# A decoder layer's block products: sums in the PSUM banks, pairs interleaved, left factors split three products ahead

## The chip, the cores and the metric

The kernel runs on one core of a Trainium2 chip. The metric is the device time of one execution in microseconds. The core has five engines with instruction queues of their own: TensorE (PE in the profile, its weight loads PEld), VectorE (DVE), ScalarE (ACT), GpSimd (POOL) and SyncE (SP), which here only issues transfers. TensorE writes its results to PSUM, eight banks of 128 x 512 f32; VectorE and ScalarE read and write PSUM, GpSimd does not in this kernel.

## The reference

One layer of a hybrid decoder on 1024 tokens of 1024 channels in f32, then a last RMS norm. What matters here, cut down:

```python
h = rmsnorm(x, norm_mix);  u = h @ w_in            # 1024 x 11264 columns, split by branch
od = diff_attention(dq, dk, dv, lam);  o_r = silu(rg) * group_norm(retention(rq, rk, rv))
o_l = rg_lru_branch(lx, ...) * gelu(ly)
g = sigmoid(gates)
merged = g[0] * (od @ w_branch[0]) + g[1] * (o_r @ w_branch[1]) + g[2] * (o_l @ w_branch[2])
x = x + merged @ w_out
x = x + cross_attention(rmsnorm(x), mem)
x = x + square(relu(rmsnorm(x) @ mlp_w1)) @ mlp_w2
return rmsnorm(x)
```

## The kernel before

Every f32 operand of a matrix product is held as the sum of two parts in the format f32r, "hi" and "lo" (`split`, L70 and L71: ScalarE casts hi, another engine subtracts to get lo). A product of two such operands is three matmuls into one PSUM bank, hi x hi, hi x lo and lo x hi (`mm3`, L59 to L61).

The kernel runs in stages: retention; differential attention; then the stage of `h_products`; the three branches' products (`branch`); the output projection (`w_out`); cross-attention; the first MLP product (`mlp_in`, `mlp1`), whose squared ReLU and the sums of its blocks go to DRAM; the second MLP product (`mlp2`).

`h_products`, `branch` and `mlp1` compute their results as 2 x 2 block products with seven multiplications instead of eight (Winograd's form). A **pair** is two weight units of 128 output channels: its four left blocks A11, A12, A21, A22 are [128, 512] each (four k-tiles of 128 channels), the right factors are blocks [128, 4, 512] of the activations, B11, B21, B22 and their sums T1 to T4, held split in SBUF in the pools slotA and slotB. The left sums are S1 = A21 + A22, S3 = A11 - A21, S2 = S1 - A11, S4 = A12 - S2 (`left`, L1067, four VectorE instructions). The products are

P1 = A11 B11, P2 = A12 B21, P3 = S4 B22, P4 = A22 T4, P5 = S1 T1, P6 = S2 T2, P7 = S3 T3,

each 4 x 3 = 12 matmuls of 512 columns, and the results C11 = P1 + P2; with U2 = P1 + P6, U3 = U2 + P7, U4 = U2 + P5: C21 = U3 + P4, C22 = U3 + P5, C12 = U4 + P3. There are 23 pairs in `h_products` (retention's gate "rg", eight LRU pairs "lru", the merge gates "gate"; from the third pair on LRU pairs and others take turns until the LRU pairs are used up), four in each of three branches, and 16 in `mlp1`: 51 pairs.

`product` takes a bank of its own for each of the seven products from six banks that take turns (`p6`). ScalarE copies P1 to the SBUF buffer t0 (L1122), VectorE makes U2, U3 and U4 in t0 and t1 (L1126, L1128, L1131) as soon as their terms are there, and `emit` gets each result block as a sum x + y still to be made: in `h_products` VectorE adds (L676) and ScalarE applies GELU or SiLU where wanted; in `branch` VectorE adds (L810), multiplies by the sigmoid of the gate (L811) and adds the sum of the branches before (L813), with the gate and that sum loaded by SP (L804, L808); in `mlp1` VectorE adds (L1147) and squares the ReLU (L1155).

The left unit of a product is split where the product is traced (`pair_unit`): hi by ScalarE, lo by GpSimd, but by VectorE for P6 and P4 in `branch` and for the first two pairs of `mlp1`. The left sums are made once P1 and P2 are traced. The raw units are loaded when P1 is traced. The order of products is ORDER = 1, 2, 6, 7, 5, 4, 3 one pair after the other, or BY_BLOCK = 1, 2, 3, 7, 6, 5, 4, which takes two pairs product by product: the first two and the last two pairs of `h_products`, pairs 2 and 3 of each branch, the first two of `mlp1`. While pairs 2 and 3 of a branch run, the right blocks of the next branch replace those that have had their last use (`load_blocks`, `fill_block`, L775: transfer, cast, lo on VectorE).

LRU pairs also run a convolution (L614, L616), the gate products with ScalarE's sigmoids, tanh, exponential and square root, and a scan on VectorE (L639 to L642). `o_sums` (L749) makes block sums of the branches' inputs on VectorE from and to DRAM.

The order within each engine's queue is made by the tile planner when the program is built: it takes the traced order as priority and its own costs of instructions to decide what is ready; `after` fixes the order of instructions that share a key, such as all casts of left units ("wsplit") and all weight loads ("wdma"). On the chip each queue is worked off in order.

```python
    def p6(self, psum):
        return lambda: psum.tile([P, HB], F32, tag="p", name="ps1", bufs=6)
```

## Time and profile before

| | |
|---|---|
| time, median of 3 executions | 2488.87 us (2486.42 to 2490.97) |
| the profiled execution's span | 2489.1 us, 31236 instructions |
| TensorE busy | 2355.3 us (95%), 11132 matmuls |
| VectorE, ScalarE, GpSimd busy | 1851.9, 1042.4, 1088.3 us (74%, 42%, 44%) |
| block products on TensorE | from 754.9 to 1556.2 and from 1821.2 to 2143.5 us; 4284 matmuls |
| bytes moved by transfers | 334.08 MB, mean 134 GB/s |

The span runs from the first to the last instruction of the profiled execution; the page gives no other time for that execution. Matmuls overlap their successors, so "busy" of TensorE is the union of rows that are each longer than the distance between two starts. In the rows of groups, "out<-in" are the program's names of tiles: `ps` a product's bank, `wu` a left unit, `block` a right factor, `sf` and `st` raw units, sums and t0, t1 in `h_products` and `branch`, `ut` and `sraw` the same in `mlp1`, `y` a branch's result, `hab` the MLP's.

### The profile page before, as it was taken

The page shows a single profiled execution, that of the slowest core. Times are in us where ns is not written, and L with a number is a line of the kernel's source. Part 1 is how long each engine was busy: PE and PEld are TensorE (multiplying, and loading weights), DVE is VectorE, ACT ScalarE, POOL GpSimd, SP SyncE. Part 2 cuts the span into 40 slices and gives each one's busy share as a digit, 9 for nine tenths or more (in the row PEclk, how much of TensorE's full clock was granted, in tenths as well). Part 3 has the DMA queues.
Part 4 walks back from the last instruction along what each step waited for, and adds up shares of the span by engine and source line. Part 5 has one row for each costly group of instructions (what it writes and reads, how often), then busy time and mean ns, then how long its engine had stood idle before and what let it go on. Part 6 is the DMA issues. An engine that isn't in the chain of part 4 may idle for free. (4 is left out here: it accounts for less than half of the span.)

```text
span 2489.1 us, 31236 instructions
## 1 busy us (share of the span) xinstructions
PE 2355.3 (95%) x11132; PEld 1906.0 (77%) x11132; DVE 1851.9 (74%) x2850; ACT 1042.4 (42%) x1823; POOL 1088.3 (44%) x714
## 2 busy tenths in 40 slices
PE   9999999999999999999998978899989999999996
PEld 7888878787876877777776767688768888778884
DVE  7577476767786777777677887534788888878888
ACT  5443344545455554454354443235442222343333
POOL 1122212221214555565553333225145555698787
PEclk9999999999999999999999989999999999999999
DMA  5222212122114435534576776434225444744432
GB/s 173 74 85 69 62 45 60 44 60 54 51 41 140 152 120 185 182 119 144 194 233 220 241 264 205 141 129 136 94 85 178 148 140 140 275 152 169 147 142 75
DMA packets 137259, 334.08 MB, mean 134 GB/s; under 512 B 17152, under 2 KB 27393, under 8 KB 137104
## 3 DMA queue, kind: packets, MB, share of 16 engines
q1 hardware_dynamic: 136528, 330.25, 40.2%
q8 instruction: 89, 1.46, 0.3%
q10 hardware_dynamic: 576, 1.84, 0.2%
q14 instruction: 66, 0.54, 0.1%
HBM read 229.21 MB, written 98.63 MB: 132 GB/s over the span
## 5 line engine op out<-in xcount | busy, mean ns | idle before, releaser
L59 PE MATMUL ps<-block,wu 128*128 128x512 f32 x1428 | 570.5, 400 | 55.6 <-DVE sf L1126 23.5
L61 PE MATMUL ps<-block,wu 128*128 128x512 f32 x1428 | 568.2, 398 | 16.7 <-POOL wu L71 10.2
L60 PE MATMUL ps<-block,wu 128*128 128x512 f32 x1428 | 565.0, 396 | 0.1
L71 POOL TENSOR_TENSOR wu<-st,wu 128x512 fp32r<-128x512 f32 x214 | 324.9, 1533 | 323.4 <-ACT wu L70 323.3
L59 PEld LDWEIGHTS ps<-block,wu 128*128 128x128 f32 x1428 | 273.2, 191 | 120.0 <-issue 19.6
L61 PEld LDWEIGHTS ps<-block,wu 128*128 128x128 f32 x1428 | 272.9, 191 | 85.5 <-POOL wu L71 15.8
L60 PEld LDWEIGHTS ps<-block,wu 128*128 128x128 f32 x1428 | 272.7, 191 | 60.7 <-DVE block L71 1.1
L70 ACT CAST wu<-st 128x512 fp32r<-128x512 f32 x240 | 141.5, 618 | 163.3 <-DVE st L1067 68.9
L59 PE MATMUL ps<-wu,hu 128*128 128x512 f32 x448 | 176.6, 394 | 15.6 <-DVE acc L1199 13.6
L71 POOL TENSOR_TENSOR w<-st,w 128x1024 fp32r<-128x1024 f32 x50 | 122.1, 2453 | 154.9 <-ACT w L70 137.5
L61 PE MATMUL ps<-wu,hu 128*128 128x512 f32 x448 | 174.9, 392 | 5.1 <-DVE hu L71 5.1
L60 PE MATMUL ps<-wu,hu 128*128 128x512 f32 x448 | 175.2, 391 | 0.1
L1199 DVE TENSOR_TENSOR acc<-acc,ps 128x512 f32<-128x512 f32 x216 | 137.8, 677 | 21.3 <-PE ps L61 20.6
L71 POOL TENSOR_TENSOR wu<-sf,wu 128x512 fp32r<-128x512 f32 x63 | 115.9, 1853 | 64.9 <-ACT wu L70 51.8
L71 DVE TENSOR_TENSOR hu<-sth,hu 128x1024 fp32r<-128x1024 f32 x56 | 122.1, 2185 | 20.6 <-ACT hu L70 20.2
L467 ACT ACTIVATE p<-sc,mx 128x256 f32<-128x256 f32 (+7 forms) x128 | 94.5, 740 | 65.8 <-DVE mx L464 61.9
L59 PEld LDWEIGHTS ps<-wu,hu 128*128 128x128 f32 x448 | 84.6, 189 | 38.9 <-DVE acc L1199 10.7
L59 PE MATMUL psk<-block,w 128*128 128x512 f32 x256 | 104.8, 409 | 0.0
L61 PEld LDWEIGHTS ps<-wu,hu 128*128 128x128 f32 x448 | 84.6, 189 | 23.5 <-DVE hu L71 6.0
L61 PE MATMUL psk<-block,w 128*128 128x512 f32 x256 | 101.8, 398 | 0.0
L60 PE MATMUL psk<-block,w 128*128 128x512 f32 x256 | 101.6, 397 | 0.0
L60 PEld LDWEIGHTS ps<-wu,hu 128*128 128x128 f32 x448 | 84.6, 189 | 17.8 <-POOL wu L71 0.5
(391 smaller groups left out, 5627.2 us busy)
## 6 DMA issues: line engine op xcount, KB each, us to landing
sth<-h SPq DMA_DIRECT2D x56, 512.0 KB, 8.9
st<-in_w SPq DMA_DIRECT2D x32, 512.0 KB, 4.3
h<-hab SPq DMA_DIRECT2D x32, 512.0 KB, 2.8
w<-in_w SPq DMA_DIRECT2D x8, 2048.0 KB
sgb<-gsp SPq DMA_DIRECT2D x48, 256.0 KB, 4.3
gsp<-l SPq DMA_DIRECT2D x44, 256.0 KB, 3.1
acc<-y SPq DMA_DIRECT2D x40, 256.0 KB, 4.2
st<-in_w_br SPq DMA_DIRECT2D x18, 512.0 KB, 6.4
```

The lines of the kernel that those rows point to most:

```text
L59: nc.tensor.matmul(ps, lhsT=lhs.hi, rhs=rhs.hi, start=start, stop=False)
L60: nc.tensor.matmul(ps, lhsT=lhs.hi, rhs=rhs.lo, start=False, stop=False)
L61: nc.tensor.matmul(ps, lhsT=lhs.lo, rhs=rhs.hi, start=False, stop=stop)
L70: ins = self.nc.scalar.copy(dst.hi, src)
L71: self.lo_ins = (lo_engine or self.nc.vector).tensor_tensor(dst.lo, src, f32(dst.hi), op=ALU.subtract)
L467: nc.scalar.activation(p[:, 0:n], sc[:, 0:n], AF.Exp, bias=mx, accum_out=l)
L1199: eng.tensor_tensor(acc[k][:, st, :], acc[k][:, st, :], x if isinstance(x, bass.AP) else acc[x][:, st, :], op=ALU.add)
```

## The change

- **Banks.** A pair has three banks instead of seven. P1 and P2 share bank X, so that it holds C11; P6, P7 and P4 share Y; P5 and P3 share Z. ScalarE copies P1 out of X to t0 before P2 is added. VectorE adds t0 to P6 in its bank (U2), ScalarE copies U2 to t0; P7 is added by TensorE (U3), ScalarE copies U3 to t1; P4 is added (C21). Z plus t1 is C22, and with P3 added to Z, Z plus t0 is C12. So `emit` gets C11 and C21 without a second term; ScalarE copies them out (in `mlp1` with ReLU and Square), and in `branch` the product with the gate reads the bank.
- **Order.** ORDER is 1, 6, 2, 5, 7, 4, 3. Neighbouring pairs overlap: P4 and P3 of a pair stand behind P1 of the next (SLOT, `overlapped`). Pairs taken product by product follow ORDER.
- **Splits ahead.** `play` prepares (loads, splits, sums) each left unit three products before its product is run. The sums S1, S3, S2 are made behind the split of A11, S4 behind that of A12, in place of the raw blocks. Lo is made on VectorE for five products, on GpSimd for P4 and P3. The next pair's raw units are loaded when P6 is prepared.
- **The rest that follows.** The T blocks of h are loaded in the order T2, T1, T3, T4, the branches' right blocks in the new ORDER; the LRU's gate products are done in two halves, behind P4 and P3 of the next pair, and use the banks of the other pool; `o_sums` stand behind P4; GpSimd makes the last add in `branch`; the last branch's blocks and the two `hx` of the output projection lie in other slots; in `mlp1` the second raw unit lies in `sraw`. The first two pairs of `mlp1` keep the old order and a bank a product (`product_apart`).

```diff
-    def mmk(self, ps, pairs):
+    def mmk(self, ps, pairs, onto=False):
         n = len(pairs)
+        kw = {"skip_group_check": True} if onto else {}
         for i, (l, r) in enumerate(pairs):
-            self.mm3(ps, l, r, i == 0, i == n - 1)
+            self.mm3(ps, l, r, i == 0 and not onto, i == n - 1, **kw)
...
-    ORDER = (1, 2, 6, 7, 5, 4, 3)
-    BY_BLOCK = (1, 2, 3, 7, 6, 5, 4)
+    ORDER = (1, 6, 2, 5, 7, 4, 3)
+    SLOT = {1: 0, 6: 3, 2: 4, 5: 5, 7: 6, 4: 8, 3: 9}
+    def overlapped(self, pairs):
+        return [x[1:] for x in sorted((7 * p + s, p, k) for p in pairs for k, s in self.SLOT.items())]
+    def play(self, seq, prep, run, ahead=3):
+        for i in range(-ahead, len(seq)):
+            if i + ahead < len(seq):
+                prep(*seq[i + ahead])
+            if i >= 0:
+                run(*seq[i])
...
+    def left_part(self, k, c, eng):
+        w, tt = c["w"], lambda o, x, y, op: eng.tensor_tensor(o, x, y, op=op)
         if k == 1:
+            tt(c["s1"], w["A21"], w["A22"], ALU.add)
+            w["S1"], w["S2"], w["S3"] = c["s1"], w["A11"], w["A21"]
+            tt(w["S3"], w["A11"], w["A21"], ALU.subtract)
+            tt(w["S2"], c["s1"], w["A11"], ALU.subtract)
+        elif k == 2:
+            w["S4"] = w["A12"]
+            tt(w["S4"], w["A12"], w["S2"], ALU.subtract)
...
+    def prepare(self, k, c, lo):
+        c["u", k] = self.pair_unit(c["w"][self.LEFT[k]], lo)
+        self.left_part(k, c, self.nc.vector)
...
+    BANK = {1: "X", 2: "X", 6: "Y", 7: "Y", 4: "Y", 5: "Z", 3: "Z"}
+    def product(self, k, c, right, psum, emit, apart=False):
+        u, r, b = c["u", k], right[self.RIGHT[k]], self.BANK[k]
+        onto = b in c
+        if not onto:
+            c[b] = psum()
+        ps = c[b]
+        self.mmk(ps, [(u[:, kt, :], r[:, kt, :]) for kt in range(4)], onto)
+        t0, t1 = c["t"]
+        if k == 1:
+            nc.scalar.copy(t0, ps)
+            if apart:
+                del c[b]
+        elif k == 2:
+            emit(0, 0, ps, None if onto else t0)
+        elif k == 6:
+            v.tensor_tensor(ps, ps, t0, op=ALU.add)
+            nc.scalar.copy(t0, ps)
+        elif k == 7:
+            nc.scalar.copy(t1, ps)
+            emit(1, 1, c["Z"], t1)
+        elif k == 4:
+            emit(1, 0, ps, None)
+        elif k == 3:
+            emit(0, 1, ps, t0)
...
     def h_products(self):
+        def prep(p, k):
+            load(p)
+            self.prepare(k, cs[p], nc.gpsimd if k in (4, 3) else v)
+            if k == 6:
+                load(p + 1)
...
+                def out(o, f=None):
+                    if y is not None:
+                        tt(o, x, y)
+                    if y is None or f is not None:
+                        nc.scalar.activation(o, x if y is None else o, f or AF.Copy)
...
-            if kind == "lru" and k == self.ORDER[5]:
+            if kind == "lru" and k == 4:
                 self.lru_conv(n, c, sp)
...
+                if k == 7:
                     self.lru_split(cs[p - 1])
+                elif k in (4, 3):
+                    self.lru_gate(jobs[p - 1][1], cs[p - 1], sp, k == 3)
-            if k == self.ORDER[2]:
+            if k == 4:
                 for i, q in sums.get(p, ()):
                     self.o_sums(i, q, sp)
...
-        for i in (3, 2, 1, 4):
+        for i in (2, 1, 3, 4):
...
+        self.play([(p, k) for k in (2, 6, 5, 7, 4, 3) for p in range(2)] + self.overlapped(range(2, m - 2)), prep, run)
...
+        self.play([(p, k) for k in self.ORDER for p in range(m - 2, m)], prep, last)
...
     def branch(self, order, i, right, bw, st, sps, nxt):
-            v.tensor_tensor(o, x, y, op=ALU.add)
-            v.tensor_tensor(o, o, sg, op=ALU.mult)
+            if y is not None:
+                z = x if (n % 2, j) == (0, 1) else o
+                v.tensor_tensor(z, x, y, op=ALU.add)
+                x = z
+            v.tensor_tensor(o, x, sg, op=ALU.mult)
             if order > 0:
-                v.tensor_tensor(o, o, pv, op=ALU.add)
+                nc.gpsimd.tensor_tensor(o, o, pv, op=ALU.add)
...
+        seq = self.overlapped(range(2))
+        seq.insert(seq.index((1, 4)), (2, 1))
+        self.play(seq + [(p, k) for k in self.ORDER for p in (2, 3) if (p, k) != (2, 1)], prep, run)
...
     def mlp1(self, p, k, c):
+            if y is None:
+                nc.scalar.activation(o, x, AF.Relu)
+                nc.scalar.activation(o, o, AF.Square)
+            else:
+                tt(o, x, y)
+                v.scalar_tensor_tensor(o, o, 0.0, o, op0=ALU.max, op1=ALU.mult)
...
+        f = self.product_apart if p < 2 else self.product
...
     def mlp_in(self):
+            self.prepare(k, cs[p], g if p > 1 and k in (4, 3) else v)
+            if (k == 6 and 1 < p < 15) or (p, k) == (1, 4):
+                self.mlp1_load(p + 1, cs[p + 1])
...
+        first = [(p, k) for k in (1, 2, 3, 7, 6) for p in range(2)] + [(0, 5), (0, 4), (1, 5), (1, 4)]
+        self.play(first + self.overlapped(range(2, 16)), prep, run)
...
-                        hx = [[self.block(s) for s in (B, A)]]
+                        hx = [[self.block(A) for _ in range(2)]]
...
-                        hx.append([self.block(A) for _ in range(2)])
+                        hx.append([self.block(s) for s in (A, B)])
```

186 lines of the change are left out of this document (90 added, 96 removed).

## The prediction

> **What bounds the kernel now.** I read the page first, then a table by stretches, then what ended TensorE's waits, then each engine inside one period.
>
> ```profile
> span 2489.1 us, 31236 instructions
> PE 2355.3 (95%) x11132; PEld 1906.0 (77%) x11132; DVE 1851.9 (74%) x2850; ACT 1042.4 (42%) x1823; POOL 1088.3 (44%) x714
> ```
>
> TensorE is the bound, but 95% says little about what is left, since a matmul's row (about 390 ns) overlaps the next one's. The stretches, with TensorE's count of instructions, show the real rate.
>
> ```profile
> core 0: us, PE busy (x) PEld busy (x) DVE busy (x) ACT busy (x) POOL busy (x), PEclk, DMA share, GB/s
> 793.40:900.00 106.60, 105.25 (x451) 85.42 (x452) 85.70 (x91) 55.22 (x80) 64.92 (x40) 0.98 0.50 163
> 900.00:1200.00 300.00, 277.52 (x1154) 220.36 (x1153) 220.66 (x240) 148.69 (x210) 177.14 (x111) 0.97 0.44 150
> 1200.00:1300.00 100.00, 97.31 (x426) 79.68 (x425) 69.93 (x79) 35.13 (x53) 49.83 (x33) 1.00 0.70 232
> 1300.00:1350.00 50.00, 49.20 (x215) 40.03 (x215) 36.98 (x44) 23.91 (x39) 18.65 (x13) 1.00 0.64 212
> 1350.00:1556.20 206.20, 175.14 (x724) 141.36 (x723) 169.13 (x206) 89.67 (x134) 71.38 (x44) 0.93 0.72 236
> 1556.20:1600.00 43.80, 33.71 (x138) 26.67 (x137) 27.60 (x29) 9.73 (x15) 12.32 (x7) 0.88 0.51 165
> 1821.20:1900.00 78.80, 68.65 (x292) 54.93 (x291) 71.02 (x95) 24.90 (x45) 45.55 (x27) 0.96 0.37 120
> 1900.00:2143.50 243.50, 243.50 (x1064) 199.35 (x1062) 198.86 (x237) 58.13 (x99) 132.12 (x86) 1.00 0.46 158
> ```
>
> The last row is the MLP's first product in its steady state and never stops: 243.5 / 1064 = 0.2288 us a matmul, 12 x 0.2288 = 2.75 us a product, 7 x 2.75 = 19.2 us a pair. At that rate the others lose: 793 to 900 106.6 - 451 x 0.2288 = 3.4; 900 to 1200 (LRU pairs alternating with gate pairs) 36.0; 1200 to 1300 2.5; 1300 to 1350 0.8; the branches 206.2 - 724 x 0.2288 = 40.5; the start of the output projection 12.2; the MLP's first two pairs about 12 (78.8 less 292 at that rate). That is some 108 us, and the change can win only there. The steady MLP, the attention and the second MLP product offer nothing of this kind.
>
> ```profile
>   DVE sf L1131: 13.3, 6
>   POOL wu L71: 9.6, 12
> ...
>   DVE sf L1126: 2.7, 1
> ...
>   DVE sf L1126: 20.8, 3
>   ACT wx L70: 5.9, 1
> ```
>
> These are what TensorE waited for (us, times): three lines from 793.5 to 1300, two from 1300 to 1560. L1131 and L1126 are VectorE sums that release a PSUM bank; POOL L71 is a late low part.
>
> ```profile
> 793.44 1.16 PE L59 MATMUL ps<-block,wu 128*128 128x512 f32 x2 [4.08 <-ACT block L70]
> ...
> 980.93 0.47 PE L59 MATMUL ps<-block,wu 128*128 128x512 f32 x1 [2.59 <-DVE sf L1131]
> ...
> 1028.13 0.47 PE L59 MATMUL ps<-block,wu 128*128 128x512 f32 x1 [2.60 <-DVE sf L1131]
> ...
> 1359.70 0.77 PE L59 MATMUL ps<-block,wu 128*128 128x512 f32 x1 [8.84 <-DVE sf L1126]
> 1360.26 0.63 PE L60 MATMUL ps<-block,wu 128*128 128x512 f32 x1
> 1360.69 0.63 PE L61 MATMUL ps<-block,wu 128*128 128x512 f32 x1
> ```
>
> The same wait returns each 1028.13 - 980.93 = 47.2 us: one LRU pair, one gate pair, and 12 gate matmuls, (84 + 84 + 12) x 0.2288 = 41.2 us of work. Behind a long wait matmuls start 0.43 us apart for a while: a stop costs more than its length.
>
> **The start, +5.5 us.** Of the first two pairs' products after P1, four need no T block before, and then P7 needs T3; in the change two need none, and then P6 needs T2, which is now loaded first. The blocks arrive at the same pace from the same moment, so the 4.08 us wait above grows by two products, 2 x 2.75. Bounds 4 to 8 (a longer stop, a slower clock behind it).
>
> **The LRU stretch, -24 us.** Two rows by engine for two periods, and the groups that matter:
>
> ```profile
> 933.10:1028.10 95.00, 87.48 (x360) 69.44 (x361) 71.29 (x79) 43.95 (x62) 54.24 (x35) 0.96 0.49 169
> ...
> L1067 DVE TENSOR_TENSOR st<-st 128x512 f32<-128x512 f32 x6 | 6.3, 1050 | 2.6 <-POOL wu L71 2.3
> L1067 DVE TENSOR_TENSOR st<-sf,st 128x512 f32<-128x512 f32 x4 | 6.0, 1488 | 18.9 <-POOL wu L71 18.9
> L1128 DVE TENSOR_TENSOR sf<-ps,sf 128x512 f32<-128x512 f32 x4 | 2.7, 682 | 0.0
> ...
> L71 POOL TENSOR_TENSOR wu<-st,wu x20: 1282/1302/2347, 941.6 to 1020.1; 128x512 fp32r<-128x512 f32 x20
> L71 POOL TENSOR_TENSOR wu<-sf,wu x9: 1283/2251/3253, 931.3 to 1026.3; 128x512 fp32r<-128x512 f32 x9
> ```
>
> VectorE works 71.29 / 2 = 35.6 us of a period and idles 11.9, of which (18.9 + 2.3) / 2 = 10.6 wait for GpSimd: the left sums overwrite raw blocks, so they stand behind GpSimd's low parts, and the next casts stand behind the sums. The change takes from VectorE, per period, U3 and U4 of two pairs (4 x 0.68, the L1128 row) and the sums of C11 and C21, which the bank now holds and ScalarE copies out (4 x 0.68): 5.4 us. It adds ten low parts. The nearest rows are the same subtraction shape: 0.69 us free (the L1067 median below), 1.05 to 1.49 in the two contended groups above; I take 0.69, as GpSimd goes from 14 low parts to 4. That is 35.6 - 5.4 + 6.9 = 37.1 us. With the other 1.3 us of idling it makes 38.4, under 41.2, and the wait for GpSimd is gone because the sums now follow VectorE's own low part. The U2 sum moves into its PSUM bank; an in-place PSUM row of 128 columns costs 0.30 us, the 512-column L1128 row 0.68, and I keep 0.68.
>
> ```profile
> L1067 DVE TENSOR_TENSOR st<-st x69: 675/693/1785, 767.1 to 2104.7; 128x512 f32<-128x512 f32 x69
> ...
> L462 DVE TENSOR_TENSOR sc<-sc,cm x128: 268/298/300, 304.9 to 758.9; 128x128 f32<-128x128 f32 x128
> ...
> L1122 ACT COPY sf<-ps x35: 567/574/616, 766.0 to 1520.5; 128x512 f32<-128x512 f32 x35
> ...
> L59 PE MATMUL ps<-block,wu x1428: 387/394/796, 754.9 to 2143.0; 128*128 128x512 f32 x179
> ...
> L70 ACT CAST wu<-st x240: 602/617/655, 689.9 to 2122.0; 128x512 fp32r<-128x512 f32 x120
> ...
> st<-in_w_gate SPq DMA_DIRECT2D x16, 512.0 KB, 4.3
> ```
>
> ScalarE gets four more copies a pair, 8 x 0.57 = 4.6 us on its 22 of a period: hidden, as long as none stands between two products of one bank (a rival below). I leave 1.9 us lost a period, for the scan's chain of ScalarE and VectorE steps, and for the block sums and the gate's two halves, which move by some products and still share two tiles; 300 / 47.4 = 6.3 periods x 1.9 = 12 of the 36 stay. Bounds 0 (VectorE still the limit) and -36.
>
> The next pair's raw loads move to the preparation of P6, four products (11 us) ahead of the first use; a load lands in 4.3 us (last row). In SP's queue each waits for the staging tile whose last reader is GpSimd's low part of S4, prepared one product earlier, and the gate stores and the loads of the block sums queue behind it: some 2 us in which nobody needs them, 0. If the load came late, ScalarE's queue would stand and rival 3's price apply. The split of three products ahead by itself costs nothing: same casts, same tiles of two units.
>
> The L1067 row shows what a GpSimd neighbour does: 0.675 us at best, 1.785 at worst, 1.1 more. The Trainium skill (SBUF — State Buffer, "Who interferes with whom") has a VectorE instruction with two SBUF inputs and a GpSimd instruction that reads SBUF shut each other out for whole instructions; the row agrees. A low part from SBUF is of that kind, so the rule speaks against moving ten of them there: if each of the four low parts of about 1.3 us left on GpSimd held VectorE for its whole length, the period would have 37.1 + 1.3 + 5.2 = 43.6 us on VectorE, the term would be -36 + 6.3 x 2.4 = about -21, and the time 3 us longer.
>
> **1200 to 1300, -1 us**: one wait of 2.7 us goes, the last pairs are re-staged. Bounds +2 and -2.5.
>
> **The branches, -25 us.** The L1126 and "ACT wx" waits (20.8 + 5.9 = 26.7) are of one kind: pairs 2 and 3 taken product by product held six banks (P3, P7, P6 of both) until VectorE made U2, and VectorE was far behind. With three banks a pair and U2 kept in its bank nothing is held so: 26.7 goes, and with it the slow starts behind four of these stops, some 2 us each by the 0.43 us spacing: about 34 of 41.
>
> What comes in its place is VectorE's lag itself, now that it makes low parts.
>
> ```profile
> 1443.55 1.23 DVE L71 TENSOR_TENSOR block<-st,block 128x1024 fp32r<-128x1024 f32 x1 [3.18 <-ACT block L70]
> ...
> 1378.90:1470.50 91.60, 79.66 (x338) 64.68 (x337) 78.21 (x95) 41.97 (x64) 32.17 (x21) 0.94 0.76 250
> ...
> L813 DVE TENSOR_TENSOR y<-y,pv 128x512 f32<-128x512 f32 x14 | 12.3, 880 | 0.0
> ...
> 1285.00:1300.00 15.00, 15.00 (x67) 12.35 (x66) 12.01 (x13) 6.90 (x10) 3.95 (x4) 1.00 0.94 320
> ```
>
> The second branch (second row): VectorE 78.2 us. Off it: sixteen adds of the earlier sum, now GpSimd's (16 x 0.88 = 14), U3 and U4 (8 x 0.68), C11 and C21 (8 x 0.68); onto it: low parts, 8 to 20 (12 x 0.69 = 8.3). So 61.7 us against 4 x 19.2 = 77 of TensorE: room, but it waits in order behind right blocks that are still loading (3.18 us in the first row). On GpSimd twelve low parts of 1.3 go and sixteen adds, priced by the same row, come: about even. Transfers: 250 GB/s x 91.6 us = 22.9 MB in 77 us is 297 GB/s, near the 320 of the last row, the best stretch. I let 9 us return at the two changes of branch: 34 - 9 = 25. Bounds 0 (all of it returns) and -41.
>
> **The output projection's start, -8 us.** Of the 12.2 us most is VectorE finishing six result blocks that the old order delivers with the last four products; the new one spreads them, and only C12 of the two pairs comes last. Left: that block's add, product, GpSimd's add, cast and low part, some 4 us, behind kt 0 to 3 (2.75 us). The blocks of hx and mT change slots; each slot comes free no later than its first write needs: 0. Bounds 0 and -11.
>
> **Seams and the MLP, +3.5 us.** Two runs end with a pair that no next pair overlaps (P7, P4, P3 in a row: 0.39 + 0.57 and an add, 1.7 us each); five runs start with three preparations at once, which the planner can hoist. Bounds 0 to 12. The MLP's first two pairs keep their order and separate banks: 0, bounds +3 and -6. The steady pairs: VectorE is busy 198.86 of 243.5 us and gets no more work (two squared ReLUs and four sums off, five low parts on), ScalarE 58 of 243.5 and four activations and two copies a pair more: hidden under TensorE, 0.
>
> **Sum**: +5.5 - 24 - 1 - 25 - 8 + 3.5 = -49 on a span of 2489.1, which is the median shown (2488.87) within 0.3: 2440.
>
> **Rivals.**
> 1. *Nearly all waits go.* For it: VectorE's sums above fit under TensorE everywhere. Against: in-order waits and the transfers' rate. LRU -36, 1200 to 1300 -2, branches -38, projection -10, with +5.5 and +2: 2489 - 78.5 = 2411.
> 2. *VectorE's lag becomes the wait for low parts.* Three products ahead is 8.2 us of cover, and the 8.84 us stop shows a lag beyond that. LRU -10, branches -8, projection -5, -1, with +5.5 and +3.5: 2474.
> 3. *Slower: the handover inside a bank.* P4 may start only when ScalarE has copied U3 out of the bank that P7 filled, one product later. From P7's last start to P4's: 0.23 + 2.75 = 2.98 us; 0.39 of matmul and 0.57 of copy leave 2.0, three casts' worth (0.62 each). P7 after P6 needs VectorE and ScalarE within two products. For it: ScalarE's chains of table loads and activations, and VectorE's lag. Against: steady pairs leave ScalarE idle most of the time. At 1.4 us for each of 51 pairs: 71 us, 2440 + 71 = 2511. It decides from 49 / 51 = 0.96 us a pair.
> 4. *It does not do what it says*: the planner already runs casts several products ahead (five in 2.7 us at 970), and what the banks free is lost again at the blocks' transfers: 2489.
>
> ```profile
> 970.26 1.13 ACT L70 CAST wu<-st 128x512 fp32r<-128x512 f32 x2
> 971.29 1.65 ACT L70 CAST wu<-sf 128x512 fp32r<-128x512 f32 x3
> ```
>
> **How the numbers follow.** Forecast 0.52, own range 2422 to 2464; rival 1 0.13; rival 2 0.18; rival 3 0.12; rival 4 0.05. A change under 0.2% (5 us) can't be told from none in a measurement of this kernel. Faster: 0.52 + 0.13 + 0.18 = 0.83 less 0.01 of rival 2's edge, 0.82; within: 0.05 and that edge, 0.06; slower 0.12. The range 2406 to 2484 holds the forecast, rival 2 and most of rival 1, and leaves out rivals 3 and 4 and little else.
>
> **What would show it.** Right: no wait for L1126 or L1131's successors before TensorE; the period near 43 us; VectorE's idle time in it no longer put down to GpSimd; the branches at 80 us; a stop of 9 to 10 us near 793. Wrong: short waits of TensorE on ScalarE's copies of PSUM in every pair (rival 3), or on VectorE's low parts in the LRU stretch and at the changes of branch (rival 2); new losses in the steady MLP.

## The result: slower by 0.6%, and the profile after

The changed kernel took 2500.99 us (median of four runs, 2500.48 to 2507.47), the kernel before on the same chip 2487.64 us (2484.72 to 2490.97). The measured ratio is 1.0062, with a 95% interval of 1.0047 to 1.0077 (the quotient of the two medians, 1.0054, lies inside it): slower, where 2440 us was forecast. Differences in microseconds below are of medians, unless they are of stretches. The profiled execution after has a span of 2498.7 us and took 2500.48.

The head of the changed kernel's page:

```profile
span 2498.7 us, 30939 instructions
PE 2362.2 (95%) x11132; PEld 1905.8 (76%) x11132; DVE 1742.5 (70%) x2817; ACT 1153.1 (46%) x2014; POOL 780.2 (31%) x525
```

VectorE works 109 us less than before, GpSimd 308 us less, ScalarE 111 us more, TensorE has the same 11132 matmuls: work moved away from VectorE and GpSimd, and the end came later all the same. Where it came from, by stages. Each boundary is the start of a stage's first matmul (or of the named product's first matmul) in the trace; the column "after, mended" is the kernel that two later edits gave, told below. Each column is one profiled execution.

| stretch, us | before | after | after, mended | forecast of the difference |
|---|---|---|---|---|
| first 7 products of h | 43.2 | 46.6 | 47.0 | +5.5 |
| to product 28 | 60.5 | 59.8 | 59.3 | |
| LRU stretch, products 28 to 126 | 322.6 | 339.8 | 318.8 | -24 |
| rest of h, to product 161 | 102.6 | 101.6 | 100.2 | -1 |
| first branch | 88.8 | 80.1 | 81.1 | -25 in the three |
| second branch | 91.5 | 94.7 | 85.0 | |
| third branch | 92.1 | 96.3 | 86.2 | |
| output projection, first half | 36.2 | 40.2 | 34.6 | -8 |
| second half, to the MLP | 228.8 | 226.5 | 226.4 | +3.5 for the seams, over all stages |
| MLP's first product, two pairs | 52.9 | 50.4 | 50.1 | |
| the other 14 pairs | 269.6 | 271.4 | 271.4 | 0 |
| MLP's second product | 332.4 | 324.3 | 324.9 | 0 |

The view by stretches on the changed kernel's own boundaries (LRU stretch, second and third branch together, start of the projection, steady MLP) has the engines' shares:

```profile
core 0: us, PE busy (x) PEld busy (x) DVE busy (x) ACT busy (x) POOL busy (x), PEclk, DMA share, GB/s
860.90:1200.60 339.70, 304.87 (x1261) 241.03 (x1260) 232.53 (x277) 194.12 (x277) 73.34 (x48) 0.96 0.43 144
...
1382.30:1573.30 191.00, 165.76 (x674) 132.26 (x673) 127.95 (x149) 86.21 (x137) 72.46 (x47) 0.93 0.69 225
1573.30:1613.50 40.20, 28.40 (x106) 21.20 (x104) 14.47 (x15) 10.20 (x14) 20.25 (x11) 0.79 0.50 160
1890.40:2161.90 271.50, 270.82 (x1178) 220.59 (x1178) 174.62 (x254) 112.52 (x196) 49.70 (x33) 1.00 0.48 164
```

No engine is full where the time was lost: in the LRU stretch VectorE is busy 233 of 340 us, in the two branches 128 of 191. That speaks for a loss of order and not of load. What TensorE waited for over the whole run (us, times, longest), in the groups of the view of waits that matter here:

```profile
PE ps L59 <- ACT sf L1179: 23.6, 13, 5.7
PE ps L59 <- ACT sf L1181: 22.3, 10, 5.8
...
PE pso L59 <- ACT block L72: 10.2, 2, 8.2
...
PE ps L59 <- DVE lx L689: 5.5, 4, 2.2
PE ps L59 <- ACT sf L1172: 5.1, 2, 2.7
```

L1179, L1181 and L1172 are the copies of U2, U3 and P1 out of the shared banks: 51.0 us in 25 stops. Of the old waits (the sums L1131 and L1126, GpSimd's low parts) none is left where banks are shared; the MLP's first two pairs, which keep a bank a product, still have one of 8.1 us. This looks like rival 3, the handover inside a bank. The experiments say that it is mostly the place at which lateness from elsewhere shows.

**What makes the copies late in the LRU stretch.** Four engines in one chain, from the changed kernel's timeline (start, duration, engine, line, operation, and the idle time before it):

```profile
1019.11 2.41 POOL L640 TENSOR_TENSOR xc<-g,xc 128x1024 f32<-128x1024 f32 x1 [21.59 <-ACT g L637]
1021.48 3.01 POOL L73 TENSOR_TENSOR wu<-st,wu 128x512 fp32r<-128x512 f32 x2
...
1023.25 1.59 SPq L1118 DMA_DIRECT2D st<-in_w_lru  x2
...
1028.94 0.69 DVE L1125 TENSOR_TENSOR sf<-st 128x512 f32<-128x512 f32 x1 [6.87 <-DMA st<-in_w_lru]
...
1042.48 1.27 DVE L618 SCALAR_TENSOR_TENSOR xc<-lx,vec,xc 128x1024 f32<-128x1024 f32 x1
...
1049.08 0.68 DVE L1178 TENSOR_TENSOR ps<-ps,sf 128x512 f32<-128x512 f32 x1
...
1049.85 0.59 ACT L1179 COPY sf<-ps 128x512 f32<-128x512 f32 x1 [1.37 <-DVE ps L1178]
...
1050.49 0.80 PE L59 MATMUL ps<-block,wu 128*128 128x512 f32 x1 [5.72 <-ACT sf L1179]
```

GpSimd's queue holds the LRU's product (L640) until ScalarE's gate is there, and the low parts behind it; the staging tile that these read is the one into which SyncE loads the next raw unit; VectorE stands 6.87 us at the left sums for that load; then it works off what piled up (scan, convolution, block sums) and reaches U2 at 1049.08. TensorE's last such stop was at 1000.50, so this period took 50.0 us; the mean over the stretch's seven periods is 339.8 / 7 = 48.5; 43 was forecast. The same in totals, from 860 to 1180: VectorE's waits for GpSimd's low parts and for the LRU's raw units before, its two largest after, and SyncE's wait for the raw units' staging tile before and after:

```profile
DVE st L1067 <- POOL wu L71: 69.3, 21, 8.8
...
DVE sf L1067 <- DMA st<-in_w_lru: 3.0, 6, 0.6
```

```profile
DVE sf L1125 <- DMA st<-in_w_lru: 40.1, 6, 11.5
DVE ps L1178 <- PE ps L61: 16.3, 5, 3.8
```

```profile
SPq L1078 <- POOL wu L71: 57.9, 17, 9.6
```

```profile
SPq L1118 <- POOL wu L73: 62.0, 20, 7.2
```

VectorE no longer waits for GpSimd's low parts directly. It waits for loads that wait for them. SyncE waited nearly as long before, so its total alone shows nothing; what is new is that VectorE stands at the end of that chain.

**What makes them late in the branches.** Again the timeline, around a stop of TensorE:

```profile
1409.52 1.30 POOL L847 TENSOR_TENSOR y<-y,pv 128x512 f32<-128x512 f32 x1
1410.79 1.29 POOL L73 TENSOR_TENSOR wu<-st,wu 128x512 fp32r<-128x512 f32 x1
...
1410.85 0.32 SPq L849 DMA_DIRECT2D acc<-y  x1
...
1412.11 0.33 SPq L1118 DMA_DIRECT2D st<-in_w_br  x1
...
1417.96 1.14 ACT L72 CAST wu<-st 128x512 fp32r<-128x512 f32 x2 [2.60 <-DMA st<-in_w_br]
...
1418.62 0.69 DVE L73 TENSOR_TENSOR wu<-st,wu 128x512 fp32r<-128x512 f32 x1 [7.10 <-ACT wu L72]
...
1419.99 1.67 POOL L847 TENSOR_TENSOR y<-y,pv 128x512 f32<-128x512 f32 x1 [6.66 <-DVE y L845]
...
1420.42 1.78 DVE L1125 TENSOR_TENSOR sf<-sf 128x512 f32<-128x512 f32 x1
1422.24 0.69 DVE L1125 TENSOR_TENSOR sf<-st,sf 128x512 f32<-128x512 f32 x1
...
1423.81 1.14 ACT L72 CAST wu<-st 128x512 fp32r<-128x512 f32 x2 [2.04 <-DVE st L1125]
...
1425.39 0.56 ACT L1181 COPY sf<-ps 128x512 f32<-128x512 f32 x1
...
1426.00 0.80 PE L59 MATMUL ps<-block,wu 128*128 128x512 f32 x1 [4.25 <-ACT sf L1181]
```

GpSimd makes an add (1409.52) and behind it the low part (1410.79) that reads the staging tile. SyncE stores the add's result (1410.85) and, as soon as the low part is done, loads the next raw unit into that tile (1412.11). ScalarE's cast of it stands 2.60 us for the landing, and VectorE's low part 7.10 us for the cast. VectorE's left sums follow, one of them 1.78 us long beside another of GpSimd's adds, and ScalarE's next cast stands 2.04 us for them. A gate and the copy of U3 come behind that cast, in one queue, and TensorE has waited 4.25 us. At the output projection's start the chain is shorter: GpSimd's last adds, ScalarE's casts of their results, TensorE (timeline of the changed kernel):

```profile
1583.71 0.62 ACT L72 CAST block<-y 128x512 fp32r<-128x512 f32 x1 [3.56 <-POOL y L847]
...
1584.38 0.79 PE L59 MATMUL pso<-wx,block 128*128 128x512 f32 x1 [8.20 <-ACT block L72]
```

### The profile page after: what moved, and what is told of

Its sections match the earlier page's. It is cut to its first block, busy times and chain, and to the rows that moved or that the text cites. A ratio compares the mean times of both kernels' runs of the same rounds, so it can differ in the third digit from the quotient of the medians.

```text
span 2498.7 us, 30939 instructions
## 1 busy us (share of the span) xinstructions
PE 2362.2 (95%) x11132; PEld 1905.8 (76%) x11132; DVE 1742.5 (70%) x2817; ACT 1153.1 (46%) x2014; POOL 780.2 (31%) x525
## 5 line engine op out<-in xcount | busy, mean ns | idle before, releaser
L73 DVE TENSOR_TENSOR wu<-st,wu 128x512 fp32r<-128x512 f32 x173 | 132.0, 774 | 67.7 <-ACT wu L72 67.6
L73 POOL TENSOR_TENSOR w<-st,w 128x1024 fp32r<-128x1024 f32 x50 | 121.5, 2441 | 149.6 <-ACT w L72 132.2
L73 POOL TENSOR_TENSOR wu<-st,wu 128x512 fp32r<-128x512 f32 x67 | 96.7, 1451 | 185.6 <-ACT wu L72 151.8
L73 DVE TENSOR_TENSOR hu<-sth,hu 128x1024 fp32r<-128x1024 f32 x56 | 124.2, 2217 | 18.6 <-ACT hu L72 18.0
L59 PEld LDWEIGHTS ps<-wu,hu 128*128 128x128 f32 x448 | 84.5, 189 | 36.2 <-DVE acc L1293 13.3
```

What stands on the lines that cost most here:

```text
L59: nc.tensor.matmul(ps, lhsT=lhs.hi, rhs=rhs.hi, start=start, stop=False, **kw)
L73: self.lo_ins = (lo_engine or self.nc.vector).tensor_tensor(dst.lo, src, f32(dst.hi), op=ALU.subtract)
```

## The experiments

All ratios are to the kernel before, measured on the same chip at the same time. "Stretch" and "branch" mean the rows of the table above, each from one profiled execution.

### First set: the handover, the order of VectorE's queue, the adds, the low parts

**A bank for each product again, in all stages**, the rest of the change kept:

```diff
-            self.product(k, c, H, psum or self.p6(sps), emit, psum is not None)
+            self.product_apart(k, c, H, psum or self.p6(sps), emit)
...
-            self.product(k, cs[p], right, self.p6(sps), lambda e, j, x, y: emit(2 * p + e, j, x, y))
+            self.product_apart(k, cs[p], right, self.p6(sps), lambda e, j, x, y: emit(2 * p + e, j, x, y))
...
-        f = self.product_apart if p < 2 else self.product
+        f = self.product_apart
```

> The changed kernel with a bank for each product and the sums U2, U3, U4, C11 and C21 on VectorE again; order, overlap, splits three products ahead and the low parts' engines stay as changed. Theory H (the loss sits in the handover inside a bank: ScalarE's copies at L1179, L1181, L1172 come late, 51 us of TensorE's waits in all): those waits go and little comes in their place; TensorE's idle time before these matmuls falls from 72 to below 45 us, the time to 2460 to 2475, a ratio of 0.990 to 0.995. Theory V (VectorE's and ScalarE's queues are late whatever the banks do, and the banks only show it): the waits come back as waits for banks or low parts, VectorE has four more sums a pair, and the time is 2490 to 2515, a ratio of 1.000 to 1.010.

Measured: 1.0051 (1.0036 to 1.0066), no different from the change. LRU stretch 331.3, branches 80.3, 98.4, 91.5, projection 46.8, second MLP product 331.0. The waits for copies are gone and others stand in their place (TensorE's waits, whole run, this kernel):

```profile
PE ps L59 <- ACT wu L72: 21.4, 2, 11.6
PE pso L59 <- ACT block L72: 16.7, 2, 14.4
PE ps L61 <- DVE wu L73: 14.7, 6, 4.5
```

So the handover is not what made the kernel slower on the whole. In the LRU stretch it has a part: without it that stretch is 8.5 us shorter, which the projection's start (+6.6) and the second MLP product (+6.7) give back. Casts and low parts are late whether or not a bank hangs on them.

**Convolution and block sums behind the next pair's U2**, so that VectorE makes U2 first:

```diff
-            if kind == "lru" and k == 4:
-                self.lru_conv(n, c, sp)
...
+                if k == 6:
+                    self.lru_conv(jobs[p - 1][1], cs[p - 1], sp)
...
-            if k == 4:
-                for i, q in sums.get(p, ()):
+            if k == 6:
+                for i, q in sums.get(p - 1, ()):
```

> The changed kernel with the LRU's convolution and the block sums of the branches' inputs moved behind U2 of the next pair, two products later. Theory H in its narrower form (U2 is late because VectorE works off the convolution and those sums first, so ScalarE's copy and P7 come late): TensorE's wait for L1179 between 800 and 1300 falls from 20.9 us to below 6 and the time by 15 to 25 us, to 2476 to 2486, a ratio of 0.996 to 1.000. Theory V: the 7 us of VectorE's work only move in front of another instruction that TensorE needs (C22 before P3, the low parts of the next products); the sum of the waits changes by less than 6 us, ratio 1.004 to 1.008.

Measured: 1.0032 (1.0020 to 1.0044); the LRU stretch 332.2, 7.6 less. TensorE's wait for the U2 copy fell from 18.7 to 2.5 us in the stretch, but the wait for the U3 copy grew from 3.0 to 7.4 and 6.9 for low parts were new: VectorE's backlog was pushed on, not cured, for it still waited 44.3 us for the LRU's raw units.

**The branches' last add back on VectorE**, one line:

```diff
-                nc.gpsimd.tensor_tensor(o, o, pv, op=ALU.add)
+                v.tensor_tensor(o, o, pv, op=ALU.add)
```

> The changed kernel with the branches' last add on VectorE again instead of GpSimd. If the late start of the output projection (TensorE loses some 21 us from 1550 to 1600, with ScalarE's casts waiting for GpSimd's adds, which stand in GpSimd's queue behind low parts of the projection's weights of 2.4 us and more) comes from that queue: that stretch loses 8 to 12 us, the time falls by 8 to 14 us, ratio 1.001 to 1.003. Rival, VectorE is then the limit there as it was before: the stretch stays within 4 us of what it is and the 32 adds cost the branches 5 us more, ratio 1.006 to 1.010.

Measured: 0.9950 (0.9935 to 0.9965), 24 us better than the change (28 by the two ratios) where 8 to 14 was expected. Second branch 86.3, third 86.3, projection 35.7: -8.4, -10.0 and -4.5, and within 1.5 us elsewhere. The term that the prediction put down as "about even" is the largest single loss.

**The kernel before with the change's low parts alone** (P3 and P4 on GpSimd, the other five on VectorE):

```diff
-            self.pair(p, k, c, units, H, psum or self.p6(sps), emit, nc.gpsimd)
+            self.pair(p, k, c, units, H, psum or self.p6(sps), emit, nc.gpsimd if k in (4, 3) else v)
...
-                      v if k in (6, 4) else nc.gpsimd)
+                      nc.gpsimd if k in (4, 3) else v)
...
-self.p6(self.mps), v if p < 2 else nc.gpsimd, emit)
+self.p6(self.mps), nc.gpsimd if p > 1 and k in (4, 3) else v, emit)
```

> The kernel before with one part of the change alone: low parts of P1, P2, P5, P6, P7 on VectorE and of P4 and P3 on GpSimd, in all three stages (from the third pair of the MLP on); order, banks and loads as before. If the wait of VectorE's left sums for GpSimd's low parts set the LRU stretch's period (the forecast's term of 24 us): the period of an LRU pair and a gate pair shrinks from 47.2 to 43 to 44 us, the time by 15 to 25 us, ratio 0.990 to 0.994. If VectorE's own chain (convolution, scan, sums, in order) sets it: the period stays within 1 us, the branches get 0 to 8 us longer, ratio 0.998 to 1.004.

Measured: 1.0001 (0.9991 to 1.0010). VectorE's 69.3 us of waiting for GpSimd in the LRU stretch are gone, its largest wait there is now 10.4 us, and the stretch took 329.7 us, 7.1 more than before. The edit also gives VectorE the low parts that the change gives it: it was busy 274.3 us there, 238.4 before. So the wait is gone, work stands in its place, and TensorE gains nothing; the run does not tell what the wait would be worth without that work. The 7.1 is not much above the spread: where its code is unchanged, the kernel before with another edit (the add alone, fourth set) took 327.1.

### Second set: all low parts of h's products on VectorE

The edit in `h_products`, beside the add on VectorE:

```diff
-            self.prepare(k, cs[p], nc.gpsimd if k in (4, 3) else v)
+            self.prepare(k, cs[p], v)
```

> The changed kernel with the branches' last add on VectorE, and in the stage of the LRU and gate pairs the low parts of P4 and P3 on VectorE too (all seven). Theory Q (a chain of queues: GpSimd's product for the LRU's gate waits for ScalarE's sigmoid, the low parts of P4 and P3 stand behind it, the staging tile stays taken, SP loads the next LRU pair's raw units late, and VectorE stands at its left sum; VectorE waits 10.6 us in 100 for that load): the wait for the load falls below 3 us in 100, the LRU stretch from 338 to 324 to 331 us, the time to 2463 to 2470, a ratio of 0.990 to 0.993. Rival L (VectorE's load sets the stretch, and two more low parts a pair add to it): the stretch is as long or up to 5 us longer, ratio 0.994 to 0.998.

Measured: 0.9876 (0.9858 to 0.9895), 2458.35 us: better than both kernels, and the "mended" column of the table. The LRU stretch fell from 338.3 to 318.8 us, more than expected, although VectorE still waits for raw units. VectorE's wait in it is 22.8 us, its longest 4.2 instead of the changed kernel's 11.5 (VectorE from 860 to 1180; then this kernel's LRU stretch, and its second and third branch together):

```profile
DVE sf L1125 <- DMA st<-in_w_lru: 22.8, 6, 4.2
```

```profile
860.70:1179.50 318.80, 297.41 (x1262) 236.03 (x1261) 244.25 (x306) 198.81 (x281) 27.56 (x20) 0.99 0.45 154
1360.80:1532.00 171.20, 160.28 (x673) 128.01 (x672) 137.49 (x180) 88.14 (x140) 31.18 (x18) 0.97 0.77 253
```

VectorE does more (244 instead of 233 us) in less time. GpSimd's queue is out of the chain to the loads; SyncE waits for the staging tile as long as before (59.9 us), but now for VectorE's own low part. A second cause is not separated from this: with GpSimd's low parts gone, VectorE's work beside it also gets shorter. With this edit alone (fourth set) the 21 convolution steps L618 take 1274 ns in the mean instead of 1570 and the seven products L647 1213 instead of 1761, together 10 us.

**The opposite edit**, low parts on GpSimd as before the change (in h, in the branches, in the MLP from the third pair on), the add on VectorE:

```diff
-            self.prepare(k, cs[p], nc.gpsimd if k in (4, 3) else v)
+            self.prepare(k, cs[p], nc.gpsimd)
...
-            self.prepare(k, cs[p], nc.gpsimd if k in (4, 3) else v)
+            self.prepare(k, cs[p], v if k in (6, 4) else nc.gpsimd)
...
-self.prepare(k, cs[p], g if p > 1 and k in (4, 3) else v)
+self.prepare(k, cs[p], g if p > 1 else v)
```

> The changed kernel with the branches' last add on VectorE and the low parts where the kernel before had them (GpSimd for all seven; in the branches VectorE for P6 and P4; the MLP's first two pairs on VectorE). The forecast had counted the move of five of seven to VectorE as the main gain of the LRU stretch; the kernel before with this move alone showed none there (7 us longer). If it is a loss there: the LRU stretch becomes 5 to 10 us shorter than 338, the rest of that stage and the branches 3 to 10 us longer, ratio 0.993 to 0.997. If it is needed with the sums in the banks (low parts late on GpSimd, left sums behind them): TensorE waits for POOL at L73 for more than 15 us, ratio 0.999 to 1.006.

Measured: 1.0143 (1.0121 to 1.0165), outside both expectations. LRU stretch 358.6. Both waits stand side by side there (VectorE, 860 to 1200, this kernel):

```profile
DVE st L1125 <- POOL wu L73: 38.9, 19, 10.5
DVE sf L1125 <- DMA st<-in_w_lru: 37.8, 6, 10.5
```

Low parts on VectorE were worth nothing to the kernel before and are worth 1.0143 - 0.9950, some 48 us, to the changed one (66 us with all seven of h). Of the 48 the LRU stretch has 20.3 and the three branches 23.1. A likely reason, argued from the order and not tested apart: the left sums now stand directly behind each split in VectorE's queue, with the next raw load behind the same tile.

**The convolution's move**, with the add on VectorE, and with the low parts too:

> The changed kernel with the branches' last add on VectorE and the convolution and block sums behind the next pair's U2. From the run with the second of these alone (LRU stretch 7.6 us shorter) and the run with the first alone (ratio 0.995): if the two do not touch each other, 2469 to 2473, ratio 0.992 to 0.994; if the shorter LRU stretch is given back later, as in the run alone where the first branch was 5 to 7 us longer, 0.994 to 0.996.

> Both at once: all seven low parts on VectorE in the stage of the LRU pairs, and the convolution and block sums behind the next pair's U2, with the branches' last add on VectorE. With the convolution moved VectorE waited 16.3 us in 100 for the LRU pair's load. Theory Q: that wait goes below 4, the LRU stretch is 315 to 322 us, shorter than the kernel before's 322.6, and the time 2452 to 2461, ratio 0.986 to 0.990. Rival L: the stretch stays at 330 or more, ratio 0.993 or more.

Measured: 0.9937 (0.9917 to 0.9958) and 0.9884 (0.9866 to 0.9901): nothing on top of 0.9950 and 0.9876 that the intervals can tell. Beside the add alone the LRU stretch is 7.1 us shorter and the first branch 4.8 longer: the gain is given back, and U2's place in the queue was a symptom.

### Third set: what each part is worth once the queues are mended

From the mended kernel (0.9876), one part undone or altered at a time. A bank for each product in all stages (the first edit above):

> The kernel with the branches' add on VectorE and all seven low parts on VectorE in the LRU pairs' stage (ratio 0.9876), with a bank for each product and U2, U3, U4, C11 and C21 summed on VectorE again. There TensorE still waited 27 us for ScalarE's copies out of shared banks. Theory H (the handover costs what its waits show): these 27 us and the slow starts behind them go, ratio 0.976 to 0.983. Rival V (four more sums a pair put VectorE behind): VectorE, busy 79 of 100 us in the LRU stretch, gets some 6 more, the waits come back as waits for low parts and banks, ratio 0.989 to 1.000. With the slower queues the same undoing changed nothing (1.0051 against 1.0062).

Measured: 0.9934 (0.9919 to 0.9949). The sums in the banks are worth some 14 us here; in the unmended kernel they were worth nothing on the whole. Without them the branches and the projection's start take 308.8 us instead of 286.9 and the second MLP product 331.1 instead of 324.9, while the LRU stretch takes 311.9 instead of 318.8.

Pairs one after the other in place of interleaved (`overlapped` returns each pair's products in ORDER):

```diff
-        return [x[1:] for x in sorted((7 * p + s, p, k) for p in pairs for k, s in self.SLOT.items())]
+        return [(p, k) for p in pairs for k in self.ORDER]
```

> The same kernel (0.9876) with the pairs one after the other in the order 1, 6, 2, 5, 7, 4, 3, without the overlap of neighbouring pairs; everything else as there. P4 now follows P7 and must wait for ScalarE's copy of U3, P3 for C22, P7 still has two products between. From the forecast's third rival: 0.39 us of matmul and 0.57 of copy, and an add, some 1 to 1.7 us a pair of TensorE's wait for L1181 and the adds, on about 39 pairs that overlapped: 40 to 65 us longer, ratio 1.003 to 1.014, also in the MLP's steady pairs, which lose nothing now. Rival (the planner fills the place with products of the next pair by itself, or the wait hides): within 8 us, ratio 0.984 to 0.991.

Measured: 0.9856 (0.9841 to 0.9871), 2452.4 us, in the rival's range and the fastest kernel of the study, though not apart from 0.9876 by the intervals. LRU stretch 308.6 (10 less), second MLP product 332.2 (7 more). TensorE's waits for U2 and U3 copies between 860 and 1180 are 3.4 us there, 14.6 with interleaving: the interleaving did not hide the handover in the LRU stretch. The edit changes one thing more: the next pair's raw units, loaded when P6 is prepared, now have six products until their first use instead of four, and VectorE's wait for the LRU's falls from 22.8 to 6.9 us. Which of the two gave the 10 us is open.

Splits one product ahead (`ahead=1` in `play`):

> The same kernel (0.9876) with the left factors prepared one product ahead instead of three. If the planner already runs casts ahead where their data are there (as in the kernel before, five casts in a row): no change beyond 5 us, ratio 0.985 to 0.990. If the place in the traced order is what sets the queues' order: TensorE waits for low parts (L73 on VectorE), behind the sums and the scan, more than 25 us in all, ratio 0.998 to 1.015.

Measured: 0.9871 (0.9844 to 0.9897). Three ahead brings nothing in this kernel.

The branches' gate loads issued three products earlier, at the preparation in place of the result:

```diff
+            if k in ENDS:
+                e, j = ENDS[k]
+                n = 2 * p + e
+                sg = sgs[n, j] = bw.tile([P, HB], F32, tag="sg", name="sgb", bufs=4)
+                nc.sync.dma_start(sg, self.gsp[i * D + n * P:i * D + (n + 1) * P, j * HB:(j + 1) * HB])
...
-            nc.sync.dma_start(sg, self.gsp[i * D + n * P:i * D + (n + 1) * P, sl])
```

> The same kernel (0.9876) with each gate block of the branches loaded three products before its use instead of at its use. If ScalarE's copies are late in the branches because its sigmoids stand in its queue waiting for those transfers (waits of 2 to 6 us for the gate's landing stand ahead of late copies): TensorE's wait for L1181 and L1172 after 1280 falls below 4 us, the three branches from 81, 85 and 86 us to 78 to 82, ratio 0.982 to 0.986. Rival (the right blocks' casts, which wait for their own transfers, or the transfers' rate set it): the branches stay within 2 us each, ratio 0.986 to 0.990.

Measured: 0.9885 (0.9867 to 0.9902), no gain: the branches take 85.3, 88.4 and 81.5 us, 2.9 more in all, and ScalarE's wait for gates went from 37.7 to 44.2 us. SyncE's queue still stood at the gates' loads for VectorE's products L845, 36.1 us where it was 33.5: a load that waits for a tile gained nothing here from an earlier place in the program.

### Fourth set: are the two faults separate, and do they exist alone?

The low parts of h alone, the adds left on GpSimd:

> The changed kernel with all seven low parts of h's products on VectorE and nothing else; GpSimd keeps the branches' last adds. If the two queue faults are separate, each in its own stage, the LRU stretch falls from 339.8 us to 316 to 322 as it did beside the moved adds, and the branches and the start of the output projection stay at the changed kernel's 80, 95, 96 and 40: 2501 less some 20, ratio 0.997 to 1.000. Rival: the two faults feed one another (the MLP weights' and right blocks' transfers shift with the stage before), and this edit alone brings much less than 20 us (1.002 or more) or much more (0.994 or less).

Measured: 0.9965 (0.9952 to 0.9978). LRU stretch 319.9, branches 78.1, 91.3, 95.9, projection 40.2. Each edit acts mostly in its own stage, and their gains nearly add up: 0.0097 for this one, 0.0112 for the add, 0.0186 for both.

The add on GpSimd alone, put into the kernel before:

```diff
-                v.tensor_tensor(o, o, pv, op=ALU.add)
+                nc.gpsimd.tensor_tensor(o, o, pv, op=ALU.add)
```

> The kernel before with one part of the change alone: the branches' last add, sixteen an order in the second and third branch, on GpSimd. Before, GpSimd makes the low parts of five of seven products there, so its queue is fuller than in the changed kernel. Theory Q (a late GpSimd low part or add holds the casts and the next blocks): at least what it costs in the changed kernel, 24 us, ratio 1.007 to 1.015, in the second and third branch and the start of the output projection. Rival: the cost exists only with the change's order of work, where results come out in a denser row; then the ratio is 0.999 to 1.003.

Measured: 1.0004 (0.9995 to 1.0014): nothing (branches 88.0, 91.9, 96.1, projection 33.4). SyncE's stores wait for GpSimd as long as they do in the changed kernel (SyncE's queue in the second and third branch, first this kernel, then the changed one):

```profile
SPq L815 <- POOL y L813: 45.5, 22, 5.0
```

```profile
SPq L849 <- POOL y L847: 48.1, 23, 6.0
```

The same lateness costs 24 us in one kernel and nothing in the other. In the kernel before, TensorE hangs on VectorE's sums there (17.9 us of waits for L1126 in this run), not on copies in ScalarE's queue, and the adds come off VectorE; that this balances the rest is a reading, not a measurement. Runs already told bear on it. The three branches and the projection's start together take, in us, each from one execution:

| | add on GpSimd | add on VectorE |
|---|---|---|
| order and banks as before | 309.4 | 308.6 |
| the change's order, a bank for each product | 317.0 | 308.8 (h's low parts on VectorE too) |
| the change's order, shared banks | 311.3 | 289.0 |

So the new order alone does not make the add dear: most of the cost, 22.3 against at most 8.2 us, needs the shared banks, where TensorE hangs on ScalarE's copies and VectorE has fewer sums to make. Which of these two it is, the runs do not separate.

The loads and stores of the block sums from GpSimd's queue instead of SyncE's:

```diff
-            self.after("hdma", nc.sync.dma_start(t[e], src[r:r + P, :].rearrange("p (j c) -> p j c", j=2)))
+            self.after("hdma", nc.gpsimd.dma_start(t[e], src[r:r + P, :].rearrange("p (j c) -> p j c", j=2)))
...
-            nc.sync.dma_start(dst[2 * e:2 * e + 2, :, q, :].rearrange("i p c -> p i c"), t[e])
+            nc.gpsimd.dma_start(dst[2 * e:2 * e + 2, :, q, :].rearrange("i p c -> p i c"), t[e])
```

> The kernel with the adds and all low parts of h's products on VectorE (2458 us, ratio 0.9876), and with the loads and stores of the block sums for the branches issued from GpSimd's queue in place of SyncE's. Theory S: VectorE's waits of 22.8 us for the LRU's raw loads between 860 and 1180 come from SyncE's queue, in which these loads stand behind block sums' loads that wait for the scan's tiles (33.2 us): the LRU stretch falls by 8 to 15 us, ratio 0.982 to 0.985. Rival T: the raw loads wait for their own staging tile (59.9 us, released by VectorE's low part): LRU stretch within 4 us of 318.8, ratio 0.986 to 0.990.

Measured: 0.9983 (0.9973 to 0.9993), 25 us worse than without the edit; LRU stretch 337.6. Theory S falls: VectorE's wait for raw units stayed at 22.1 us. GpSimd now stands at waiting loads and stores, with the LRU's products behind them: once more, little work in a queue that waits.

The branches' P3 and P4 low parts on VectorE too:

> The kernel with the adds and all low parts of h's products on VectorE (2458 us, ratio 0.9876), and with the branches' low parts of P4 and P3 on VectorE too. If late GpSimd low parts are what is left of the branches' loss (252 us for 756 matmuls a branch and pair set that would take 231), the three branches fall by 6 to 12 us, ratio 0.982 to 0.986. Rival: VectorE, which also makes the branches' low parts of right blocks, adds and products, is the later engine there, and the eight more low parts a branch (8 x 0.69 = 5.5 us) are paid: the branches grow by 3 to 15 us, ratio 0.989 to 0.994.

Measured: 0.9872 (0.9857 to 0.9887). Branches 82.8, 83.6, 84.9: neither expectation, no change.

### Fifth set: does SyncE's queue carry the branches' lateness?

The store of a branch's result issued from GpSimd's queue, right behind its add; and the same with the add on VectorE:

```diff
-                nc.sync.dma_start(self.acc[order][rows, sl], o)
+                nc.gpsimd.dma_start(self.acc[order][rows, sl], o)
```

> The changed kernel; only the branches' stores of their results are issued from GpSimd's queue, behind its own add, in place of SyncE's queue, where they wait 48.1 us for GpSimd's adds between 1382 and 1573 with the next raw units, gates and earlier sums behind them. Theory SQ (SyncE's queue carries GpSimd's lateness to the loads, these to ScalarE's casts and so to its copies of the banks): the second and third branch and the start of the output projection fall from 94.7, 96.3 and 40.2 us by 10 to 24 in all, ratio 0.996 to 1.002. Rival GQ: the add itself is too late or the issue from GpSimd costs as much: within 6 us of the changed kernel, ratio 1.004 to 1.009.

> The changed kernel with the branches' adds on VectorE (0.995) and the same stores from GpSimd's queue, which has nothing else to do there but the low parts of P4 and P3. The price of the store's issue from GpSimd alone: nothing if the queue was not the matter here (0.993 to 0.997), up to 10 us more if GpSimd's low parts now stand behind stores that wait for VectorE (0.997 to 1.000), and some us less if the 29.3 us that SyncE's queue still waits for VectorE's adds held loads (0.989 to 0.993).

Measured: 1.0055 (1.0038 to 1.0071) and 1.0011 (1.0000 to 1.0022). The first is not different from the change (second branch 92.6, third 96.2, projection 39.9), the control is 14 us worse than its own base (0.9950); in the control GpSimd's low parts stand behind stores that wait for VectorE. The wait did not leave SyncE's queue, it went to the next entry: the loads of the earlier sums (L839) need the tile that GpSimd's add reads (SyncE's queue, 1382 to 1573, first run):

```profile
SPq L835 <- DVE y L845: 46.4, 14, 8.1
SPq L839 <- POOL y L847: 39.6, 25, 3.2
```

So theory SQ is neither shown nor refuted: no run with the adds on GpSimd took their lateness out of SyncE's queue.

## Why the prediction was wrong, point by point

**The bound.** TensorE is the bound, and the steady MLP behaved as forecast: 269.6 and 271.4 us, with VectorE at 175 instead of 225 us, ScalarE at 113 instead of 65, and the banks' handover hidden.

**The start, +5.5 us.** Right in kind and too large: the stop grew from 4.08 to 6.42 us (row below, the changed kernel's timeline), the first seven products by 3.4 us, under the lower bound of 4.

```profile
789.66 0.80 PE L59 MATMUL ps<-block,wu 128*128 128x512 f32 x1 [6.42 <-ACT block L72]
```

**The LRU stretch, -24 us: wrong in sign, +17.2.** The sum set VectorE's work in a period, 37.1 us, and 1.3 of other idling against TensorE's 41.2. The work came out even smaller, 232.53 / 7 = 33.2 us, and the period was 48.5: it was set by waits in order, which the sum priced at 1.9 us. Three steps failed.

The first is "VectorE works 71.29 / 2 = 35.6 us of a period and idles 11.9", of which 10.6 of waiting for GpSimd was read as time to win. In the kernel before, with the low parts moved, these waits were gone and the stretch was no shorter (329.7 against 322.6).

The second is the raw loads at 0, "some 2 us in which nobody needs them". The step named the very chain (the staging tile's last reader is GpSimd's low part of S4, prepared one product earlier) and then priced it by the load's landing of 4.3 us alone. VectorE's left sums need the load at once, and they stand in front of the scan, the convolution and U2: 40.1 us of waiting in the stretch, where it was 3.0. With the low parts of P4 and P3 of h on VectorE the stretch is 318.8, a gain of 3.8 on before; that the low parts on GpSimd cost some 20 us is shown, and how much of it goes through the loads is not (the wait only fell to 22.8, and VectorE's other work got shorter too).

The third is rival 3's price, put at nothing in the sum as "hidden". In the LRU stretch a bank for each product takes 8.5 us off the changed kernel and 6.9 off the mended one, and pairs in sequence, whose raw units also come earlier, take 10.2 off the mended one: 308.6, -14 on before. The -24 exists in no run.

**1200 to 1300, -1 us.** Measured -1.0 (102.6 to 101.6); that it is so near is luck, for two later kernels with the same code there, the mended one and the one with earlier gate loads, took 100.2 and 104.4.

**The branches, -25 us: -1.3.** "26.7 goes" was right: the waits for L1126 and the wx casts are gone. But waits for the copies L1181, L1172 and L1179 came, 19.0 + 5.1 + 2.7 = 26.8 us from 1302 to 1620. The first branch, without earlier sums to add, gained 8.7 us all the same. In the other two "twelve low parts of 1.3 go and sixteen adds, priced by the same row, come: about even" failed. By load it holds: GpSimd is busy 72 us in them, 64 before. By order it does not: the add is the last step of a result, and behind it stand stores, loads, gates, casts and, in ScalarE's queue, the copies that the shared banks had just made TensorE wait for. Back on VectorE the three branches take 80.7, 86.3 and 86.3 us, 19.1 less than before: most of the -25. So one instruction's engine accounts for most of what this term missed.

That the add costs 24 us in the changed kernel and nothing in the kernel before (1.0004) is shown; the stretches say that most of it needs the shared banks. Through which queue is not: the chain above is the trace's, and the run that should have cut it left the wait in place.

**The output projection's start, -8 us: +4.0.** The same add. "Left: that block's add, product, GpSimd's add, cast and low part, some 4 us" counted one block; GpSimd's adds stood among its low parts of the projection's weights, and ScalarE's casts of their results waited 2.7 to 3.7 us for five of six. On VectorE the stretch is 35.7, -0.5; the -8 was too much in any case.

**Seams and the MLP, +3.5 us.** At the MLP's last pair, the one seam that the rows show apart, TensorE waited 0.7 us for the copy of U3 where 1.7 was put. The rest of the projection to the MLP's start (-2.3) was in no term; the first two pairs (-2.5) stay inside their bounds. Not in the sum at all: the second MLP product, -8.1 us.

**Three ahead "by itself costs nothing".** It costs nothing, and it wins nothing: in the mended kernel one ahead is as fast. This is rival 4's argument, for this part alone.

**The rivals.** Rival 3 was the one on the right side, and its sign came, short stops at the copies, in 25 places with 51.0 us. Its mechanism did not decide: without shared banks the kernel takes the same time (1.0051), and with the queues mended the shared banks gain 14 us. Only in the LRU stretch does the handover cost what it was said to in kind, 7 to 8.5 us. Rival 2's waits for low parts come to 14.7 us with separate banks and to less than 1 us in the changed kernel. Rival 1 fell. The outcome, both sums of waits moving along the queues, was on no list; the chance of 0.12 for slower belonged to a price of the handover alone, so that the time came out on that side is no merit of it.

**The rule on VectorE and GpSimd.** The row at 1420.42 above, a sum of two SBUF tiles in 1.78 us beside GpSimd's add at 1419.99, against 0.69 for the next one alone, is of the size that the prediction quoted. The Trainium skill (SBUF — State Buffer, "Who interferes with whom") has such pairs exclude each other; the trace agrees. The period that the rule gave in the prediction, 43.6 us of VectorE's work, did not come, for VectorE worked 33.2. The rule's effect is in the rows all the same: in the LRU stretch every L618 and L647 of more than 1.5 us lies beside one of GpSimd's subtractions L73, and without the low parts of P4 and P3 there these rows got 10 us shorter in all.

**The signs named.** No wait for the sums before TensorE: seen. A period near 43 us: 50.0 in the one shown. VectorE's idle time no longer put down to GpSimd: seen, and it won nothing. Branches at 80 us: the first only. A stop of 9 to 10 us near 793: 6.42. Waits on the copies, the sign of rival 3: seen, though in 25 places and not in every pair.

## What to carry to other kernels

Before moving an operation to an idle engine, follow what stands behind its result in each in-order queue: the same add cost nothing in one kernel and 24 us in another, and GpSimd was the less busy in the one where it cost (72 of 191 us in the two branches, 104 of 188 where it was free). Idle time of an engine off the bound can be worth nothing: ask whether the bounding engine waits for its end. A wait removed in the middle of a chain can come back at the next entry, as with separate banks, the moved convolution, the moved low parts and the moved stores here. When a change of many parts loses, try the small ones first: two edits of one line each took this one from 1.0062 to 0.9876.
